# A hybrid decoder layer: the second tiles' turns through three PSUM banks, w_down differences tied to the products, attention's groups of products kept whole

## The chip, the cores and the metric

The kernel runs on one core of one Trainium2 chip. The time is that of one execution on the device, in microseconds, as the median of a few runs. Engines are named as in the profile: PE is TensorE (matrix products), PEld its weight loads, DVE is VectorE, ACT is ScalarE, POOL is GpSimd, SP is SyncE, which issues most DMA transfers.

## The reference, cut to what matters

One layer on 2048 tokens of width 1024, all float32: attention in a window of 128 tokens and a convolution group side by side, one output projection, then a gated feed-forward network of width 2816.

```python
h = x
hn = rms_norm(h, mix_pre_g)
proj = hn @ w_in                       # q (8 heads of 64), k, v (2 heads), u
attn_out = sliding_window_attention(q, k, v, attn_sinks, rel_bias)
conv_out = conformer_conv(u, conv_dw, conv_dw_b, conv_ln_g, conv_ln_b, w_conv_pw)  # width 31
mixed = jnp.concatenate([attn_out, conv_out], axis=-1) @ w_out
h = h + rms_norm(mixed, mix_post_g)
hn = rms_norm(h, ffn_pre_g)
ff = (jax.nn.silu(hn @ w_gate) * (hn @ w_up)) @ w_down
h = h + rms_norm(ff, ffn_post_g)
```

Inside the attention, for each block of 128 queries: scores against 256 keys (the block before and its own), a bias by distance, a mask, a softmax with a sink for each head, and the product with the values.

## The kernel before

The 2048 tokens are four tiles of 512. A float32 operand of a product is split into a rounded part and a rest (ACT writes the first, a subtraction on DVE the second), and a product is three: first by first, first by rest, rest by first. That is why products come in threes and twelves.

The stages, by the letter behind the @ in a tile's name, with the tile's number (A1 is stage A of tile 1): A projects the inputs, tile by tile; B is attention; C is the convolution, whose 31 taps are multiply-adds on DVE; U folds the pointwise weight into the output projection; W is the output projection and the norm behind it. The feed-forward network works on pairs of tiles (0 with 1, 2 with 3) and by Strassen's scheme: seven products of half size for eight. H makes its operands from the normed rows: for the first tile of a pair plain (`stage_h_plain`), for sums and differences of the quarter blocks in `stage_h_sums`, which needs the second tile's rows too. F makes gate and up: first those of the seven products that need no sums (`stage_pre`; some results are stored in `keeps` and loaded again to seed a bank, line 939), then the others (`stage_p1`), which can start when the operand sums and the first weight sums are there. G is the product with w_down (`stage_p2`). Its weights need differences of w_down's blocks. `stage_tsums` makes the first four of them ahead of time: it loads four blocks (line 1106), subtracts on DVE, and stores the results (line 1112), all its transfers on POOL's queue, in eleven sets.

Attention takes one tile in four blocks. `front` makes the scores of a block in two halves: twelve products of half the array's rows (64 x 128, for two heads at a time) into two banks of PSUM, then a masked copy and two reductions for each bank on DVE. `back` of the block before turns the probabilities on PE (line 491), ACT takes them out of PSUM, POOL cuts them to the window (line 494), and four products of half the array's columns (128 x 64) make the output.

PSUM has eight banks: four named mm for the big products, three named tr, and one named ct. Attention's scores, turns and outputs use tr in rotation. The turns of the normed rows (`turn_row`, eight a tile, four transposes each, line 816) use ct; ACT empties the bank behind each.

A scheduler sets each engine's order at build time. It knows the dependencies, follows a timeline of its own with estimated times, and of the instructions that are ready takes the one with the lowest priority number, which is by default the place in the program's text. Lanes (`Lane.pump`) pull a step of a side stage (attention, taps, tail, operand sums, w_down differences) into the text of the main stage whenever it has gained credit. `tc.add_manual_dep` adds a dependency by hand: of the class NoSync it only sets the order, of the class Sync the engine also waits for it on the chip. The taps were already tied to products in that way (`dve`). Each engine runs its list in order.

Of the kernel before, what the change touches and what calls it, by code (L numbers as in the profile page):

```python
# [37 lines left out]
def layer_kernel(ctx, tc, x, xT, cols, rows, sinks, relb, onehot, w_in, w_pw, w_out, w_gate, w_up, w_down, out):  # L38
    nc = tc.nc
# [21 lines left out]
    def f2(tag, shape=(P, T)):  # L61
        return t_(tag, shape)
# [110 lines left out]

    def after_first(first, r):
        tc.add_manual_dep(
            r.ins,
            first.ins.name,
            mybir.DependencyInfo(mybir.DependencyClass.NoSync, mybir.DependencyReason.DATA),
            reason="both halves of the array start together",
        )  # L180
# [62 lines left out]
    hT = [dr.tile([KC, P, T], F32, name=f"hT{i}") for i in range(2)]  # L243
    qs = {}
    started = set()

# [75 lines left out]
    def stage_a(t, hn, before_kv, hooks, post=None):  # L322
# [79 lines left out]
        for i in range(4):  # L402
# [9 lines left out]
            if post:  # L412
                qt = f2("fa")
                stt(qt, oq, 0.125, rb, ALU.mult, ALU.mult)
                act(qi[:, 0], qt, AF.Copy)
                vtt(qi[:, 1], qt, qi[:, 0].bitcast(F32), ALU.subtract)
            else:
                act(qi[:, 0], oq, AF.Copy, scale=0.125)
                stt(qi[:, 1], oq, 0.125, qi[:, 0].bitcast(F32), ALU.mult, ALU.subtract)
            q.append(qi)  # L420
            yield 5.2
            step(10 + i)
        qs[t] = q

    def stage_b(t):
# [3 lines left out]
        def front(b):  # L429
# [6 lines left out]
            for ip in range(2):  # L436
                os = [tr().rearrange("p (j k) -> p j k", j=2) for _ in range(2)]
                lead = []
                for j in range(2):
                    i = 2 * ip + j  # L440
                    for n, (a, k) in enumerate(((0, 0), (0, 1), (1, 0))):
                        for g in (1, 0):
                            sl = slice(64 * g, 64 * g + 64)
                            r = mat(os[g][:, j], q[i][sl, a, tok], kz[sl, k, win], start=n == 0, stop=n == 2)
                            if lead:
                                after_first(lead[-1], r)
                            if len(lead) < 2:
                                lead.append(r)
                for g in range(2):
                    prev = neg.unsqueeze(2).to_broadcast([P, 2, P]) if first else os[g][:, :, 0:P]  # L450
                    nc.vector.copy_predicated(os[g][:, :, P:], upper.unsqueeze(1).to_broadcast([P, 2, P]), prev)
                    for j in range(2):
                        h = 4 * g + 2 * ip + j
                        nc.vector.tensor_tensor_reduce(
                            out=pr[:, h],
# [24 lines left out]
        def back(b):  # L480
# [3 lines left out]
            for g in range(2):  # L484
# [8 lines left out]
                for kb in range(1 if first else 0, 2):  # L493
                    nc.gpsimd.affine_select(  # L494
                        out=pg[:, kb].rearrange("p (i q) -> p i q", q=P),
# [11 lines left out]
            o = tr()  # L507
            lead = None
            for kb in (1,) if first else (1, 0):
                for g in (1, 0):  # L510
                    sl = slice(64 * g, 64 * g + 64)
                    r = mat(o[sl], vtok[:, b + kb, sl], pt[g][:, kb], start=kb == 1, stop=first or kb == 0)
                    if lead is None:
                        lead = r
                    else:
                        after_first(lead, r)
            at = f2("at")
            act(at, o, AF.Copy)
# [5 lines left out]

        live = {}
        for b in range(5):
            if b < 4:
# [284 lines left out]
    def turn_row(w, xs, k, u):  # L812
        lab[0] = f"H{w}"
        b = ct()
        for s in range(4):
# [283 lines left out]
    def stage_tsums(td):  # L1099
        L = "G0"  # L1100
        for pr in range(NF // 2):
# [248 lines left out]
    RP = 0.1  # L1350
    TIE = 5
    AHEAD = 3
    PRES = {0: 20, 2: 16}
# [172 lines left out]
```

## Time and profile before

| what | value |
|---|---|
| median of 3 runs | 1982.09 us (1979.29 to 1984.77) |
| the profiled execution | 1987.9 us, span 1986.2 us |
| PE busy | 1930.4 us, 97% |
| DVE, ACT, POOL busy | 74%, 48%, 15% |
| mean granted clock of PE | 0.987 of full speed |

The profile is of one execution. "Busy" is the time in which an engine carried out instructions; a row of the timeline gives start, duration, engine, line, operation, output <- inputs, shape of the tile in the array, and the number of like instructions in a row, and in brackets the idle time ahead of it and what ended it. A row of the windows gives start:end and length, then busy time and number of instructions of PE, PEld, DVE, ACT and POOL, then the mean granted clock, the busy share of the DMA engines, and GB/s. A row of the waits gives the engine's instruction and what it waited for: us in total, times, longest. Attention runs from about 98 to 590 us, the first half's F stage from about 600 to 1010, its G stage to about 1320, the second half's F and G stages from there to the end.

### The profile page before, as it was taken

Reading aid. Unit: us, or ns where it says so; the run is one execution under the profiler, and the core shown is the slowest. Engines: PE = TensorE matmul, PEld = TensorE weight load, DVE = VectorE, ACT = ScalarE, POOL = GpSimd, SP = SyncE. Lnnn points to the kernel's source line nnn. Section 1 sums busy time; section 2 is a strip of 40 time slices with the busy share of each in tenths; the row PEclk is TensorE's granted clock in tenths of the full one; section 3 lists DMA queues with packets and bytes.
Section 4 is the critical chain, followed back from the end, with each engine's and each line's share of the span. In section 5 each row is a group of like instructions: output and inputs, shape, how many; then the busy total and the mean of one; then the engine's idle time right before and its main releaser. Section 6 shows DMA issues by size and latency. Waiting matters only on the chain.

```text
span 1986.2 us, 26652 instructions
## 1 busy us (share of the span) xinstructions
PE 1930.4 (97%) x8730; PEld 1546.7 (78%) x8730; DVE 1476.3 (74%) x2648; ACT 961.8 (48%) x1886; POOL 304.3 (15%) x427
## 2 busy tenths in 40 slices
PE   8999999999999699999999999999899999999997
PEld 6877777777777588778888878887688888888886
DVE  5999969995874899787759965666866775555557
ACT  5455354447647544334345464656533433345443
POOL 4011011111121101220000110000023332311003
PEclk9999999999999799999999999999899999999999
DMA  8787657566658668775478777759844542375664
GB/s 311 251 303 219 210 187 256 185 212 214 225 195 281 232 218 266 260 266 184 130 253 276 259 255 242 249 202 309 293 140 169 179 140 96 132 244 181 211 195 144
DMA packets 209578, 435.67 MB, mean 219 GB/s; under 512 B 21752, under 2 KB 39328, under 8 KB 209440
## 3 DMA queue, kind: packets, MB, share of 16 engines
q1 hardware_dynamic: 191648, 402.52, 60.7%
q0 software_dynamic: 7040, 23.07, 3.5%
q10 hardware_dynamic: 10752, 8.39, 1.3%
q8 instruction: 68, 1.11, 0.2%
q14 instruction: 70, 0.57, 0.1%
HBM read 323.26 MB, written 110.63 MB: 218 GB/s over the span
## 4 chain that ended last, share of the span: by engine, by line
PE 77%; DVE 8%; DMA 7%; issue 3%; POOL 2%; ACT 2%; SPq 0%; DVEq 0%; POOLq 0%; ACTq 0%
PE mm@F L85 32%; PE mm@G L85 16%; PE mm@A L85 15%; PE mm@W L85 4%; PE tr@B L85 4%; PE tr@W L85 2%; DVE fc@C L94 2%; DMA wx@G<-w_down 1%; DMA gb@F<-keeps 1%; PE mm@U L85 1%; DVE w@F L94 1%; DVE hl@G L94 1%; PE tr@B L491 1%; DMA td<-wx@G 1%; DMA fc@G<-w_down 1%
## 5 line engine op out<-in xcount | busy, mean ns | idle before, releaser
L94 DVE SCALAR_TENSOR_TENSOR fc@C<-glu@C,colt,fc@C 128x512 f32<-128x512 f32 x480 | 357.3, 758 | 2.6
L85 PE MATMUL mm@F<-hl@H,w@F 128*128 128x512 f32 x1056 | 261.3, 397 | 10.2 <-ACT mm@F L939 10.2
L85 PEld LDWEIGHTS mm@F<-hl@H,w@F 128*128 128x128 f32 x1056 | 201.0, 192 | 54.6 <-ACT mm@F L939 12.5
L85 PE MATMUL mm@G<-hl@G,hl@G 128*128 128x512 f32 x924 | 227.7, 393 | 1.1 <-DVE hl@G L94 1.1
L821 ACT ACTIVATE w@F<-chl@F 128x512 fp32r<-128x512 f32 x220 | 135.9, 626 | 187.8 <-PE mm@F L85 149.6
L85 PE MATMUL mm@A<-hl@A,w@A 128*128 128x512 f32 x840 | 209.5, 397 | 4.2 <-ACT w@A L127 1.5
L85 PEld LDWEIGHTS mm@G<-hl@G,hl@G 128*128 128x128 f32 x924 | 171.7, 188 | 37.3 <-DVE hl@G L94 1.9
L85 PE MATMUL mm@G<-w@G,hl@G 128*128 128x512 f32 x876 | 199.4, 389 | 0.0
L85 PEld LDWEIGHTS mm@G<-w@G,hl@G 128*128 128x128 f32 x876 | 164.4, 188 | 34.1
L85 PEld LDWEIGHTS mm@A<-hl@A,w@A 128*128 128x128 f32 x840 | 156.6, 189 | 42.9 <-issue 3.3
L94 DVE TENSOR_TENSOR w@F<-chl@F,w@F 128x512 fp32r<-128x512 f32 x198 | 151.4, 768 | 49.0 <-ACT w@F L821 48.8
L85 PE MATMUL mm@F<-mid@H,w@F 128*128 128x512 f32 x528 | 136.5, 398 | 20.3 <-ACT w@F L821 13.3
L85 PEld LDWEIGHTS mm@F<-mid@H,w@F 128*128 128x128 f32 x528 | 101.0, 192 | 43.7 <-ACT w@F L821 14.1
L85 PE MATMUL mm@F<-ql@H,w@F 128*128 128x512 f32 x528 | 130.0, 392 | 0.0
L85 PE MATMUL mm@F<-p@H,w@F 128*128 128x512 f32 x528 | 129.1, 389 | 0.0
L85 PE MATMUL mm@F<-x@H,w@F 128*128 128x512 f32 x528 | 126.9, 391 | 0.0
L85 PEld LDWEIGHTS mm@F<-ql@H,w@F 128*128 128x128 f32 x528 | 99.1, 189 | 20.8
L85 PEld LDWEIGHTS mm@F<-p@H,w@F 128*128 128x128 f32 x528 | 99.1, 188 | 20.6
L85 PEld LDWEIGHTS mm@F<-x@H,w@F 128*128 128x128 f32 x528 | 98.4, 188 | 21.1 <-issue 0.8
L127 ACT ACTIVATE w@A<-raw@A 128x512 fp32r<-128x512 f32 x110 | 67.5, 626 | 92.1 <-PE mm@A L85 62.1
L94 DVE TENSOR_TENSOR w@G<-raw@G,w@G 128x512 fp32r<-128x512 f32 x73 | 52.1, 713 | 73.0 <-ACT w@G L821 71.8
L494 POOL TENSOR_SCALAR_AFFINE_SELECT p@B<-p@B 128x512 f32<-128x512 f32 x62 | 51.7, 843 | 338.4 <-ACT p@B L492 337.1
(314 smaller groups left out, 3290.1 us busy)
## 6 DMA issues: line engine op xcount, KB each, us to landing
mids<-fa@F SPq DMA_DIRECT2D x154, 256.0 KB, 2.7
raw@A<-w_in SPq DMA_DIRECT2D x55, 512.0 KB, 4.6
w@A<-lo_in SPq DMA_DIRECT2D x84, 256.0 KB, 3.3
fc@G<-mids SPq DMA_DIRECT2D x77, 256.0 KB, 3.4
fa@G<-mids SPq DMA_DIRECT2D x75, 256.0 KB, 4.4
gb@F<-keeps SPq DMA_DIRECT2D x72, 256.0 KB, 3.5
w@W<-fold SPq DMA_DIRECT2D x32, 512.0 KB, 5.9
raw@F<-w_gate SPq DMA_DIRECT2D x22, 512.0 KB, 4.0
```

Source lines behind the costliest of these rows:

```text
L85: r = nc.tensor.matmul(*args, **kw)
L94: r = op(*args, **kw)
L127: act(w[:, 0], raw, AF.Copy)
L491: nc.tensor.transpose(o[:, i * P : (i + 1) * P], pr[:, 4 * g + i], ident)
L494: nc.gpsimd.affine_select(out=pg[:, kb].rearrange("p (i q) -> p i q", q=P), in_=pg[:, 1].rearrange("p (i q) -> p i q", q=P), compare_op=AL ...
L821: act(w[:, 0], x, AF.Copy)
```

## The change

It has three parts. The turns of tiles 1 and 3 (`w % 2`) go through the three tr banks rather than through ct. Each of the w_down subtractions gets an order dependency on the last big product that the text holds at that place. And attention's groups are kept together: each group of score products, and each of output products, gets a higher priority by SOON = 100, its first product comes behind the last product of the group before, and waits (Sync) on what would make it stop midway: for a score group the previous half's last reduction of the first bank and, in a tile's first block, the second query split it reads; for an output group the last affine_select.

```diff
+    def after_first(first, r, how="NoSync"):
...
+            mybir.DependencyInfo(getattr(mybir.DependencyClass, how), mybir.DependencyReason.DATA),
...
             for ip in range(2):
...
+                before = group[0]
+                p0 = tc.cur_priority
+                tc.cur_priority = p0 - SOON
...
                             if lead:
                                 after_first(lead[-1], r)
+                            else:
+                                for e, how in ((before, "NoSync"), (scored[0], "Sync"), (None if b else q_ready[t][2 * ip + 1], "Sync")):
+                                    if e is not None:
+                                        after_first(e, r, how)
                             if len(lead) < 2:
                                 lead.append(r)
+                            group[0] = r
+                tc.cur_priority = p0
...
+                        if g == 0 and j == 1:
+                            scored[0] = e
...
+            tc.cur_priority = p0 - SOON
             for kb in (1,) if first else (1, 0):
...
                     if lead is None:
                         lead = r
+                        after_first(group[0], r)
+                        after_first(cut, r, "Sync")
...
     def turn_row(w, xs, k, u):
         lab[0] = f"H{w}"
-        b = ct()
+        b = tr() if w % 2 else ct()
...
-                vtt(o, p_, q_, ALU.subtract)
+                r = vtt(o, p_, q_, ALU.subtract)
+                tc.add_manual_dep(
+                    r.ins,
+                    made["rows"][-1].name,
+                    mybir.DependencyInfo(mybir.DependencyClass.NoSync, mybir.DependencyReason.DATA),
+                    reason="weight differences keep pace with the products",
+                )
...
+    SOON = 100
```

Attention, PE's order around the output products of a block of tile 2 (`tr@B2_605`) and the first score products of the next block (`tr@B2_609` and `tr@B2_610`, with kz for the keys); before:

```order
L85 MATMUL mm@W0_620_3874<-w@W0_616_3846,hl@W0_593_3706 128x512 x3
L85 MATMUL tr@B2_605_3779<-p@B2_587_3673,vtok_112 64x512
L85 MATMUL tr@B2_610_3790<-kz_109,ql@A2_492_3120 128x256
L85 MATMUL tr@B2_605_3779<-p@B2_585_3663,vtok_112 64x512
L85 MATMUL tr@B2_609_3789<-kz_109,ql@A2_492_3120 128x256
L85 MATMUL tr@B2_605_3779<-p@B2_587_3673,vtok_112 64x512
L85 MATMUL tr@B2_610_3790<-kz_109,ql@A2_492_3120 128x256
L85 MATMUL tr@B2_609_3789<-kz_109,ql@A2_492_3120 128x256
L85 MATMUL tr@B2_605_3779<-p@B2_585_3663,vtok_112 64x512
L85 MATMUL tr@B2_610_3790<-kz_109,ql@A2_492_3120 128x256
L85 MATMUL tr@B2_609_3789<-kz_109,ql@A2_492_3120 128x256
L85 MATMUL tr@B2_610_3790<-kz_109,ql@A2_499_3181 128x256
```

and now, the same two groups:

```order
L85 MATMUL mm@W0_639_3973<-w@W0_637_3961,hl@W0_593_3706 128x512
L85 MATMUL tr@B2_605_3779<-p@B2_587_3673,vtok_112 64x512
L85 MATMUL tr@B2_605_3779<-p@B2_585_3663,vtok_112 64x512
L85 MATMUL tr@B2_605_3779<-p@B2_587_3673,vtok_112 64x512
L85 MATMUL tr@B2_605_3779<-p@B2_585_3663,vtok_112 64x512
L85 MATMUL tr@B2_610_3790<-kz_109,ql@A2_492_3120 128x256
L85 MATMUL tr@B2_609_3789<-kz_109,ql@A2_492_3120 128x256
L85 MATMUL tr@B2_610_3790<-kz_109,ql@A2_492_3120 128x256
L85 MATMUL tr@B2_609_3789<-kz_109,ql@A2_492_3120 128x256
L85 MATMUL tr@B2_610_3790<-kz_109,ql@A2_492_3120 128x256
L85 MATMUL tr@B2_609_3789<-kz_109,ql@A2_492_3120 128x256
L85 MATMUL tr@B2_610_3790<-kz_109,ql@A2_499_3181 128x256
```

Before, the eight records of two groups alternate one by one; now the four output products stand in a row, and the twelve score products behind them.

PE's order around the turns of tile 1's rows (`@H1`, one name for each of eight rows; `mm@F0` are the big products of the F stage, three to a row of the list); before:

```order
L85 MATMUL mm@F0_1022_6159<-hl@H0_810_4970,w@F0_1008_6098 128x512 x3
L85 MATMUL mm@F0_1022_6159<-hl@H0_813_4981,w@F0_1008_6098 128x512 x3
L816 MATMUL ct@H1_974_5934<-ident_69,chl@W1_938_5731 128x128
L816 MATMUL ct@H1_974_5934<-ident_69,chl@W1_939_5733 128x128
L816 MATMUL ct@H1_974_5934<-ident_69,chl@W1_940_5735 128x128
L816 MATMUL ct@H1_974_5934<-ident_69,chl@W1_941_5737 128x128
L85 MATMUL mm@F0_1022_6159<-hl@H0_821_5028,w@F0_1008_6098 128x512 x3
L85 MATMUL mm@F0_1028_6191<-hl@H0_802_4927,w@F0_1013_6125 128x512 x3
L85 MATMUL mm@F0_1028_6191<-hl@H0_810_4970,w@F0_1013_6125 128x512 x3
L85 MATMUL mm@F0_1028_6191<-hl@H0_813_4981,w@F0_1013_6125 128x512 x3
L85 MATMUL mm@F0_1028_6191<-hl@H0_821_5028,w@F0_1013_6125 128x512 x3
L85 MATMUL mm@F0_1034_6218<-hl@H0_802_4927,w@F0_1020_6154 128x512 x3
```

and now, from the fourth of the eight turns on:

```order
L85 MATMUL mm@F0_1016_6133<-hl@H0_810_4970,w@F0_1000_6062 128x512
L836 MATMUL tr@H1_979_5962<-ident_69,chl@W1_938_5731 128x128
L836 MATMUL tr@H1_979_5962<-ident_69,chl@W1_939_5733 128x128
L836 MATMUL tr@H1_979_5962<-ident_69,chl@W1_940_5735 128x128
L836 MATMUL tr@H1_979_5962<-ident_69,chl@W1_941_5737 128x128
L85 MATMUL mm@F0_1016_6133<-hl@H0_810_4970,w@F0_1000_6062 128x512
L836 MATMUL tr@H1_981_5969<-ident_69,chl@W1_938_5731 128x128
L836 MATMUL tr@H1_981_5969<-ident_69,chl@W1_939_5733 128x128
L836 MATMUL tr@H1_981_5969<-ident_69,chl@W1_940_5735 128x128
L836 MATMUL tr@H1_981_5969<-ident_69,chl@W1_941_5737 128x128
L836 MATMUL tr@H1_985_5994<-ident_69,chl@W1_938_5731 128x128
L836 MATMUL tr@H1_985_5994<-ident_69,chl@W1_939_5733 128x128
```

Before, the turns 974 and 979 have eight rows, 23 products, between them, and the last turn (`ct@H1_993`) stands beside the product `mm@F0_1081`; now three turns stand together in the product `mm@F0_1016`, and the last two ahead of `mm@F0_1028`.

DVE's order ahead of the first weight of the middle products (`w@F0_1104`; `fa` are results of F products, `@H0` the operand sums, `fc@C2` and `glu@C2` taps, `wx@G0` and `fc@G0` w_down differences); before:

```order
L94 TENSOR_TENSOR mb@H0_1070_6406<-chl@H0_1066_6379,mb@H0_1070_6406 128x512
L94 TENSOR_TENSOR mid@H0_1055_6327<-chl@H0_1036_6239,mid@H0_1055_6327 128x512
L94 TENSOR_TENSOR chl@F0_1102_6596<-chl@F0_1101_6594 128x512
L94 TENSOR_TENSOR chl@H0_1059_6351<-chl@H0_1059_6351,chl@H0_1066_6379 128x512
L94 TENSOR_TENSOR wx@G0_1119_6658<-fc@G0_1121_6660,wx@G0_1119_6658 128x512
L94 TENSOR_TENSOR ql@H0_1071_6409<-chl@H0_1066_6379,ql@H0_1071_6409 128x512
L94 SCALAR_TENSOR_TENSOR fc@C2_1083_6465<-glu@C2_1082_6463,colt_74,fc@C2_1083_6465 128x512
L94 TENSOR_TENSOR p@H0_1077_6436<-chl@H0_1059_6351,p@H0_1077_6436 128x512
L94 TENSOR_TENSOR chl@F0_1103_6599<-raw@F0_1100_6592,chl@F0_1101_6594 128x512
L94 TENSOR_TENSOR chl@F0_1102_6596<-chl@F0_1102_6596,raw@F0_1100_6592 128x512
L94 TENSOR_TENSOR w@F0_1104_6602<-chl@F0_1102_6596,w@F0_1104_6602 128x512
L94 TENSOR_TENSOR fc@G0_1121_6660<-fc@G0_1121_6660,wx@G0_1119_6658 128x512
```

and now:

```order
L94 TENSOR_TENSOR fa@F0_1076_6434<-fa@F0_1076_6434,mm@F0_1075_6420 128x512
L94 TENSOR_SCALAR fc@C2_1083_6465<-glu@C2_1082_6463,colt_74 128x512
L94 TENSOR_TENSOR chl@H0_1059_6351<-chl@H0_1059_6351,chl@H0_1066_6379 128x512
L94 TENSOR_TENSOR w@F0_1092_6517<-raw@F0_1085_6471,w@F0_1092_6517 128x512
L94 TENSOR_TENSOR ql@H0_1071_6409<-chl@H0_1066_6379,ql@H0_1071_6409 128x512
L94 TENSOR_TENSOR p@H0_1077_6436<-chl@H0_1059_6351,p@H0_1077_6436 128x512
L94 TENSOR_TENSOR chl@F0_1102_6596<-chl@F0_1102_6596,raw@F0_1100_6592 128x512
L94 TENSOR_TENSOR chl@F0_1103_6599<-raw@F0_1100_6592,chl@F0_1101_6594 128x512
L94 SCALAR_TENSOR_TENSOR fc@C2_1083_6465<-glu@C2_1082_6463,colt_74,fc@C2_1083_6465 128x512
L94 TENSOR_TENSOR w@F0_1104_6602<-chl@F0_1102_6596,w@F0_1104_6602 128x512
L94 TENSOR_TENSOR fa@F0_1088_6490<-fa@F0_1088_6490,mm@F0_1087_6476 128x512
L94 TENSOR_TENSOR mid@H0_1078_6439<-chl@H0_1059_6351,mid@H0_1078_6439 128x512
```

Before, that weight stands 54 instructions behind the addition `fa@F0_1076` and behind `fa@F0_1088`, `1095` and `1099`; now it stands nine behind `fa@F0_1076` and ahead of the others, and the first w_down subtraction (`wx@G0_1116`) comes 15 rows behind it.

More of the change, by code (lines that the diff above doesn't have):

```diff
@@ L177, in after_first @@
             first.ins.name,
-            mybir.DependencyInfo(mybir.DependencyClass.NoSync, mybir.DependencyReason.DATA),
-            reason="both halves of the array start together",
+            mybir.DependencyInfo(getattr(mybir.DependencyClass, how), mybir.DependencyReason.DATA),
+            reason="products of half the array stand together",
         )
```

15 lines of the change are left out of this document (10 added, 5 removed).

## The prediction

> **What bounds the kernel now.** I read the page first, then the PE timeline for stalls, then windows and waits around each stall.
>
> ```profile
> span 1986.2 us, 26652 instructions
> ...
> PE 1930.4 (97%) x8730; PEld 1546.7 (78%) x8730; DVE 1476.3 (74%) x2648; ACT 961.8 (48%) x1886; POOL 304.3 (15%) x427
> ...
> PE   8999999999999699999999999999899999999997
> ...
> PE 77%; DVE 8%; DMA 7%; issue 3%; POOL 2%; ACT 2%; SPq 0%; DVEq 0%; POOLq 0%; ACTq 0%
> ```
>
> TensorE sets the time: it is busy for 97% and is 77% of the chain that ended last. So a gain must either shorten TensorE's own work or remove one of its pauses. Only two slices dip inside the span, the 14th (about 645 to 695 us) and the 29th (about 1390 to 1440 us). The profiled execution took 1987.9 us, 5.8 above the median of 1982.1; I sum against the former and carry the difference to the latter.
>
> **Attention (98 to 590 us): groups kept whole.** Windows of this stage, then TensorE's pieces on its timeline (start, duration, count):
>
> ```profile
> 98.00:248.00 150.00, 150.00 (x755) 114.83 (x754) 143.70 (x337) 77.09 (x196) 16.82 (x28) 1.00 0.75 245
> 298.00:448.00 150.00, 150.00 (x705) 111.28 (x704) 142.24 (x304) 69.92 (x183) 18.86 (x23) 1.00 0.67 218
> 98.00:590.00 492.00, 492.00 (x2391) 366.82 (x2390) 421.62 (x952) 260.66 (x642) 73.19 (x137) 1.00 0.67 221
> ```
>
> ```profile
> 104.30 0.50 PE L85 MATMUL mm@A<-mid@A,w@A 128*128 128x512 f32 x1
> 104.73 0.38 PE L85 MATMUL tr@B<-kz,ql@A 64*128 64x256 f32 x1
> 105.04 0.50 PE L85 MATMUL mm@A<-mid@A,w@A 128*128 128x512 f32 x1
> ...
> 225.15 1.29 PE L85 MATMUL mm@A<-hl@A,w@A 128*128 128x512 f32 x5
> 226.38 0.97 PE L85 MATMUL tr@B<-kz,ql@A 64*128 64x256 f32 x12
> 227.28 0.96 PE L85 MATMUL mm@A<-hl@A,w@A 128*128 128x512 f32 x3
> ...
> 259.89 1.07 PE L85 MATMUL tr@B<-p@B,vtok 128*64 128x512 f32 x2
> 260.89 0.38 PE L85 MATMUL tr@B<-kz,ql@A 64*128 64x256 f32 x1
> ```
>
> ```profile
> 201.66 1.94 PE L85 MATMUL tr@B<-p@B,vtok 128*64 128x512 f32 x8
> 203.53 1.67 PE L85 MATMUL mm@A<-hl@A,w@A 128*128 128x512 f32 x6
> ```
>
> TensorE never idles here (492.00 of 492.00), so cost is the distance from start to start. A full product costs 0.227: 67 steps of it and a last product of 0.50 make the 15.69 us of the row of 68 below. Twelve score products together take 227.28-226.38 = 0.90, plus 0.09 on the product ahead (225.15 to 226.38 is 1.23, five products are 1.14): 0.99, or 0.08 each. One alone takes 105.04-104.73 = 0.31 and lengthens the product ahead from 0.227 to 0.43. A whole value group (eight records, four products) takes 203.53-201.66 = 1.87, and I give it the same 0.09; one product alone (two records) takes 260.89-259.89 = 1.00, so four alone would be 4.0. These groups are now in 72 score pieces and 29 value pieces, first to last:
>
> ```profile
> L85 PE MATMUL tr@B<-kz,ql@A x384: 272/277/385, 98.4 to 559.9; 64*128 64x256 f32 x192
> L85 PE MATMUL tr@B<-p@B,vtok x124: 592/592/644, 145.5 to 585.7; 128*64 128x512 f32 x124
> ```
>
> Summed start to start, with what they add to the product ahead, the score pieces cost 45.9 us and the value pieces 40.3. After the change the order has 35 score pieces and 16 whole value groups: 32 x 0.99 plus some 0.7 for three splits is 32.4, and 15 x 1.96 plus 1.1 for the short first group is 30.5. That is 86.2-62.9 = 23.3; walking TensorE's two orders with the same step costs gives 22.7 (3.7 of it at 98 to 248 us, 7.7 at 298 to 448). Nothing hides it, since TensorE is the busy engine. What can eat it is that heads wait (Sync) for the last reduction and the last affine_select, with everything behind them on TensorE held. VectorE is 143.70 of 150 and 142.24 of 150 busy, so those stretches could shrink by 6.3 and 7.8 before it is the bound, against 3.7 and 7.7 asked. Bounds: -24 (all), and -11 (only the 22.7-11.4 outside the two stretches). I take **-20**, near the full end, because TensorE waits nowhere in this stage now.
>
> [...]
>
> **The start of the middle products (656 to 697 us).** The second tiles' turns went through one bank, a turn for about each 24 products; the operand sums on VectorE come behind them.
>
> ```profile
> 645.05 0.60 PE L816 MATMUL ct@H<-ident,chl@W 128*128 128x128 f32 x4
> ...
> 650.74 0.60 PE L816 MATMUL ct@H<-ident,chl@W 128*128 128x128 f32 x4
> ...
> 656.80 15.69 PE L85 MATMUL mm@F<-hl@H,w@F 128*128 128x512 f32 x68
> 685.10 1.22 PE L85 MATMUL mm@F<-mid@H,w@F 128*128 128x512 f32 x2 [12.61 <-ACT w@F L821]
> 689.31 2.08 PE L85 MATMUL mm@F<-mid@H,w@F 128*128 128x512 f32 x4 [3.00 <-DVE w@F L94]
> 691.19 2.76 PE L85 MATMUL mm@F<-mb@H,w@F 128*128 128x512 f32 x6
> 693.75 3.55 PE L85 MATMUL mm@F<-ql@H,w@F 128*128 128x512 f32 x12
> ```
>
> ```profile
> 655.73 0.69 DVE L94 TENSOR_TENSOR fa@F<-fa@F,mm@F 128x512 f32<-128x512 f32 x1 [0.89 <-PE mm@F L85]
> ```
>
> ```profile
> 625.00:672.00 47.00, 47.00 (x220) 38.89 (x219) 29.13 (x46) 31.43 (x55) 1.99 (x4) 1.00 0.75 251
> 655.70:688.60 32.90, 18.00 (x78) 14.05 (x77) 32.87 (x55) 16.67 (x28) 4.84 (x9) 0.79 0.68 230
> 672.24:697.14 24.90, 9.29 (x27) 6.69 (x26) 24.90 (x41) 8.97 (x15) 5.38 (x10) 0.59 0.65 218
> ```
>
> The 68 products end at 656.80 + 68 x 0.227 = 672.24. VectorE then is busy without a gap (32.87 of 32.90): sums, taps and w_down differences stand ahead of the weights' splits. The next 24 products (2, 4, 6 and 12) take from there to 697.14, 24.9 us instead of 5.45, most of them at a lower clock (mean 0.59): 19.4 lost. In the new order all second turns are issued within some 27 products, the sums begin about 25 us earlier, and the first weight for the middle products stands nine VectorE instructions behind the fa addition of 655.73; at 32.90/55 = 0.60 us each it is there near 662, ten before TensorE needs it. The w_down differences stand behind it. I take **-18.5** of 19.4; the other end is 0, if VectorE's work is only shifted. The cover: the sums lie in VectorE's gaps of 625 to 672 us, 29.13 of 47 busy. There 37 instructions now stand between two fa additions four blocks apart, a block being the 5.69 from turn to turn above; 37 x 0.60 = 22.2 against 22.8 us of TensorE's time, so that cover is thin. Splits that come late there, and the normed rows' loads asked for sooner, cost 0 to 9 (half of the loss they remove); I put **+4**. The pause near 613 us stays:
>
> ```profile
> 615.53 6.69 PE L85 MATMUL mm@F<-hl@H,w@F 128*128 128x512 f32 x21 [2.14 <-ACT mm@F L939]
> ```
>
> **The w_down differences (800 to 880 us).** Their set of four subtractions waits on VectorE, which is in order, for its loads:
>
> ```profile
> 811.83:826.03 14.20, 9.73 (x35) 7.47 (x35) 14.16 (x23) 4.42 (x8) 4.10 (x8) 0.88 0.76 263
> 875.45 2.43 PE L85 MATMUL mm@F<-ql@H,w@F 128*128 128x512 f32 x10
> 879.40 1.66 PE L85 MATMUL mm@F<-yt@H,w@F 128*128 128x512 f32 x6 [1.53 <-DVE at@F L94]
> ```
>
> ```profile
> DVE wx@G L94 <- DMA wx@G<-w_down: 9.1, 3, 6.5
> ```
>
> 34 products take 14.2 instead of 7.7 us at 812, ten take 3.95 instead of 2.27 at 875: 6.5+1.7 = 8.2 lost. Tied to the products, the sets stand 14 to 46 VectorE rows apart from the end of one to the start of the next (mean 26; before, 14 to 23, mean 18). Eight rows more are about 5 us, against a longest wait of 6.5. I take **-6.5**; ends -8.2, and 0 if the loads are late by as much. The first set's first subtraction, which stood in attention, moves behind the start of the middle products too, and the last ends some 20 us later, still ahead of the down products. Their DMAs are the same number on POOL's queue.
>
> **The second half's seeds (1372 to 1438 us).** The fourth tile's turns move too, and with them two loads of 512 KB on SP's queue, ahead of seeds.
>
> ```profile
> 1372.59:1437.86 65.27, 53.70 (x211) 41.73 (x209) 50.02 (x87) 35.83 (x65) 4.71 (x1) 0.90 0.88 312
> 1430.06 4.64 PE L85 MATMUL mm@F<-mid@H,w@F 128*128 128x512 f32 x10 [2.81 <-DVE w@F L94]
> chl@H<-hT SPq DMA_DIRECT2D x3, 512.0 KB, 4.4
> ```
>
> On its timeline these are 195 products, 44.3 us of work, and turns for about 1.1; 65.3 passed: 19.9 lost, some 7 of it around the late split of 1430, the rest behind seeds that DMA (0.88 busy) brings late. Earlier sums take the latter; two loads of 4.4 us ahead of seeds may add 8.8. I take **-4** (ends -7 and +9).
>
> Sum: -20-18.5+4-6.5-4 = **-45**: 1942.9 for a profiled execution, 1937 for the median.
>
> **The rivals.** [...] B: the start stays late; the turns come sooner but the sums push splits and seeds back where VectorE's cover is 0.6 us, so that half of 18.5 and the differences' gain go: -45+9+6.5 = -29.5, 1953. For it: the 12.61 pause followed a VectorE without a gap. C: the two loads crowd the seeds at 0.88 DMA: -45+13 = -32, 1950. D, slower: each of 48 group heads stalls TensorE for its bank, reduction or affine_select, because the planner's times differ from the chip's. The price is 48 x the wait; it decides from 45/48 = 0.94 us per head, and 1.2 us each give 1937+58 = 1995. The pause of 2.14 above shows that longer ones cost double: 21 products took 6.5 instead of 4.8. Against D: the heads have 2.7 us or more of VectorE work in hand in the new order, except one with 0.6. [...] E: the groups and ties bring waits as long as what they take: no change.
>
> **How the numbers follow.** Forecast 0.58, A 0.13, B 0.13, C 0.08, D 0.06, E 0.02. About 6 us (0.3%) is what a measurement of this kernel can tell from no change. All but D and E are faster: 0.92; E 0.02; D 0.06. The range goes from all ends together, -24-19.4-8.2-6.8 = -58 (1924), with 2 below for the spread of runs, to B with attention at -11 and the seeds unimproved, about -17 (1965).
>
> **What would show it.** Right: score pieces of 12 and value pieces of 8 on TensorE's timeline and no pause before them; the 14th slice at 9 and clock 9; no wait for w_down above 1 us; the 29th slice as it was or better. Wrong: TensorE waiting for VectorE's reductions or for POOL in 98 to 590 us; a pause at the middle products; seeds waited for longer than 20 us in all around 1350 to 1400.

## The result and the profile after

The changed kernel takes 1955.2 us (median of 4 runs, 1951.4 to 1960.1), the kernel before 1983.4 beside it: a ratio of 0.9856 with a 95% interval of 0.9834 to 0.9878, some 28 us less. The forecast was 45 less, 1937, in a range of 1922 to 1965.

The page of the changed kernel, its head, slices and chain:

```profile
span 1949.7 us, 26646 instructions
...
PE 1902.9 (98%) x8730; PEld 1537.4 (79%) x8730; DVE 1475.9 (76%) x2648; ACT 958.6 (49%) x1886; POOL 299.0 (15%) x427
...
PE   8999999999999999999999999998999999999997
...
PE 67%; DVE 15%; DMA 10%; issue 4%; ACT 2%; POOL 2%; SPq 1%; DVEq 0%; POOLq 0%; ACTq 0%
```

The 14th slice is full now; the other dip (the 28th slice, about 1316 to 1365 us) is as it was. TensorE is busy for 27.5 us less, some 23 of them in attention, and VectorE's share of the chain nearly doubled, from 8 to 15%.

Attention, as windows (the first two as before, the last cut to where VectorE is fullest), then TensorE's waits in it, then pieces of its timeline:

```profile
98.00:248.00 150.00, 148.86 (x769) 116.20 (x768) 144.75 (x337) 77.96 (x198) 18.11 (x29) 1.00 0.74 250
298.00:440.00 142.00, 138.72 (x695) 105.76 (x694) 138.73 (x307) 68.73 (x180) 21.58 (x28) 1.00 0.67 215
```

```profile
PE mm@W L85 <- DVE x@W L94: 2.1, 1, 2.1
PE tr@B L85 <- DVE sm@A L94: 1.1, 1, 1.1
PE mm@A L85 <- DVE x@W L94: 0.7, 1, 0.7
```

```profile
374.48 1.94 PE L85 MATMUL tr@B<-p@B,vtok 128*64 128x512 f32 x8
376.35 0.97 PE L85 MATMUL tr@B<-kz,ql@A 64*128 64x256 f32 x12
377.25 4.62 PE L85 MATMUL mm@W<-w@W,hl@W 128*128 128x512 f32 x19
384.01 1.65 PE L85 MATMUL mm@W<-w@W,hl@W 128*128 128x512 f32 x6 [2.15 <-DVE x@W L94]
```

A value group of eight records and a score group of twelve stand whole, at the 1.87 and 0.90 us read before. TensorE waited for nothing here before. Now one wait (1.1 us) is at the head of a group; the others shown are projections that wait for VectorE's additions.

The start of the first half's middle products, and TensorE's window there:

```profile
627.85 25.11 PE L85 MATMUL mm@F<-hl@H,w@F 128*128 128x512 f32 x108 [0.83 <-ACT mm@F L959]
652.80 1.30 PE L85 MATMUL mm@F<-ql@H,w@F 128*128 128x512 f32 x5
...
672.71 2.36 PE L85 MATMUL mm@F<-yt@H,w@F 128*128 128x512 f32 x6 [2.29 <-DVE at@F L94]
674.86 2.45 PE L85 MATMUL mm@F<-mid@H,w@F 128*128 128x512 f32 x6
```

```profile
640.00:690.00 50.00, 46.92 (x199) 37.92 (x198) 46.37 (x76) 23.18 (x42) 8.60 (x16) 0.97 0.80 264
```

The middle products follow at 652.80 without a pause. A smaller one comes 20 us later, where VectorE, busy for 46.37 of 50, is late with an addition. VectorE's waits from 600 to 900 us:

```profile
DVE fa@F L94 <- DMA mids<-fa@F: 10.3, 6, 3.1
DVE wx@G L94 <- DMA fc@G<-w_down: 6.4, 3, 3.2
...
DVE wx@G L94 <- DMA wx@G<-w_down: 1.7, 1, 1.7
```

The longest wait for w_down fell from 6.5 to 3.2 us, and all of them together from 16.2 to 8.1; the sign that the prediction asked for, none above 1 us, did not come. The waits for stores of fa, 2.8 us in the same window before (2.0 in a second look at that kernel), have grown to 10.3. The second half's seeds:

```profile
1341.07 7.57 PE L85 MATMUL mm@F<-hl@H,w@F 128*128 128x512 f32 x24 [2.65 <-ACT mm@F L959]
1353.74 8.43 PE L85 MATMUL mm@F<-hl@H,w@F 128*128 128x512 f32 x24 [5.10 <-ACT mm@F L959]
...
1372.55 23.66 PE L85 MATMUL mm@F<-hl@H,w@F 128*128 128x512 f32 x96 [1.96 <-ACT mm@F L959]
1396.05 2.88 PE L85 MATMUL mm@F<-mid@H,w@F 128*128 128x512 f32 x12
```

Here the middle products (1396.05) start on time too, and the pauses for seeds are longer instead: 12.1 us in all and up to 5.10, where they were 8.1 and the longest 3.3.

To see where time went, I took the starts of the same few products from each trace and list the distance between them (us). The columns are: start of the 341st product of A (before attention's groups); to the last of W; to the 694th of F (over the start of the middle products); to the 1387th of F (over the w_down differences); to the second half's 1849th; to the 2311th (over the seeds); to the end.

```
                      start  attention  mid start  w_down  ...G...  seeds   rest
before                 96.5      475.5      167.9   165.4    416.5  128.2  536.1
before, second look    97.8      475.5      164.8   163.3    417.4  128.4  536.0
after                  97.4      456.8      152.2   162.0    417.3  128.1  536.0
turns alone            97.1      475.5      153.4   164.6    417.3  124.7  536.3
ties alone             97.5      475.6      161.3   166.9    419.2  126.1  536.2
groups alone           97.2      457.9      167.1   167.6    417.4  124.9  536.4
tile 3's turns in ct   97.0      460.4      149.9   162.1    418.3  127.2  536.4
without ties           96.9      460.4      154.2   167.8    417.9  124.9  536.1
without waits          96.9      468.2      152.4   161.7    419.1  125.9  536.1
differences on POOL    97.9      457.7      159.4   178.9    417.3  123.8  536.2
fewer taps             97.0      456.2      149.6   163.1    417.1  127.5  536.2
taps later, t3 in ct   98.7      459.7      149.2   165.5    423.3  130.6  536.2
seeds sooner, t3 in ct 97.4      457.0      147.4   161.3    420.1  128.4  536.4
seeds sooner, t3 in tr 96.4      458.8      146.4   163.5    417.6  118.1  536.2
```

Where attention's groups are as before, and TensorE waits for nothing there, attention takes the same time in every trace (475.5, 475.5, 475.5, 475.6). With whole groups it doesn't: five kernels with one and the same order of TensorE in this stretch (after, tile 3's turns in ct, differences on POOL and both with seeds sooner) take 456.8 to 460.4. Most of that spread stands behind the two longest pauses, where products run at half speed in some traces and not in others (0.43 us apart instead of 0.227); behind the pause at 119 us they do so in tile 3's turns in ct (1.62 us long) and not in the changed kernel (1.14). So the 456.8 of the changed kernel is the shortest of the five. Behind attention a stretch differs by 3 us and more from execution to execution of the same code (the first and the second look at the kernel before: 167.9 and 164.8).

### The profile page after: what moved, and what is told of

It is laid out like the page before. It is cut to its first block, busy times and chain, and to the rows that moved or that the text cites. A ratio compares the mean times of both kernels' runs of the same rounds, so it can differ in the third digit from the quotient of the medians.

```text
span 1949.7 us, 26646 instructions
## 1 busy us (share of the span) xinstructions
PE 1902.9 (98%) x8730; PEld 1537.4 (79%) x8730; DVE 1475.9 (76%) x2648; ACT 958.6 (49%) x1886; POOL 299.0 (15%) x427
## 4 chain that ended last, share of the span: by engine, by line
PE 67%; DVE 15%; DMA 10%; issue 4%; ACT 2%; POOL 2%; SPq 1%; DVEq 0%; POOLq 0%; ACTq 0%
PE mm@F L85 30%; PE mm@G L85 17%; PE mm@A L85 8%; DVE fc@C L94 5%; PE mm@W L85 4%; PE tr@W L85 3%; PE tr@B L85 2%; DMA mids<-fa@F 2%; DVE w@F L94 1%; DMA keeps<-fa@F 1%; DVE chl@F L94 1%; DVE fa@F L94 1%; DMA w@W<-fold 1%; DMA gb@F<-keeps 1%; PE tr@B L504 1%
## 5 line engine op out<-in xcount | busy, mean ns | idle before, releaser
L85 PE MATMUL mm@F<-hl@H,w@F 128*128 128x512 f32 x1056 | 261.1, 398 | 14.8 <-ACT mm@F L959 13.6
L85 PEld LDWEIGHTS mm@F<-hl@H,w@F 128*128 128x128 f32 x1056 | 201.1, 192 | 61.6 <-ACT mm@F L959 17.7
L841 ACT ACTIVATE w@F<-chl@F 128x512 fp32r<-128x512 f32 x220 | 136.3, 626 | 186.3 <-PE mm@F L85 164.8
L507 POOL TENSOR_SCALAR_AFFINE_SELECT p@B<-p@B 128x512 f32<-128x512 f32 x62 | 56.6, 918 | 338.1 <-ACT p@B L505 336.6
```

Of the source, the lines that this page charges most:

```text
L85: r = nc.tensor.matmul(*args, **kw)
L507: cut = nc.gpsimd.affine_select(out=pg[:, kb].rearrange("p (i q) -> p i q", q=P), in_=pg[:, 1].rearrange("p (i q) -> p i q", q=P), compare ...
L841: act(w[:, 0], x, AF.Copy)
```

## The experiments

**One part at a time.** My theory was that the parts add up, each at its place; the rival, that the w_down differences in VectorE's queue, not the sums, made the long pause.

Turns alone:

```diff
 # the kernel before
-        b = ct()
+        b = tr() if w % 2 else ct()
```

> The kernel before with the turns of tiles 1 and 3 in the three tr banks, and nothing else. Theory (the parts add up, each at its place): the middle products of the first half start without the long pause, -14 at 656 to 697 us; the seeds of the second half lose what the earlier sums gain there, 0; attention as before, 0; the w_down waits stay, 0. Sum -14, about 1969. Rival (the w_down differences ahead of the splits were the cause of the long pause): the pause stays mostly, -3, about 1980.

1970.5 us, ratio 0.9936 (0.9920 to 0.9952). The start of the middle products takes 153.4 instead of 167.9, 14.5 less, as the theory had it. The rival falls: three subtractions of w_down still run in the 40 us ahead of the first of the middle products (five before), and the long pause is gone; TensorE's longest wait in this stretch is 1.7 us. The next run is the counterpart: none runs there, and a long pause stays.

Ties alone:

```diff
 # the kernel before
-                vtt(o, p_, q_, ALU.subtract)
+                r = vtt(o, p_, q_, ALU.subtract)
+                tc.add_manual_dep(r.ins, made["rows"][-1].name, ...)
```

> The kernel before with the w_down differences tied to products, and nothing else. Theory: five instructions of 0.60 us less ahead of the first split, 3 us of the long pause, and 3.5 us of the waits at 800 to 880 us: -6, about 1977. Rival: the pause was due to the differences, -14 to -18, about 1967. Third: the waits for w_down only move, with nothing gained, 0.

1984.9 us, ratio 1.0004 (0.9993 to 1.0016): nothing, the third case. The long pause is shorter, 9.60 instead of 12.61:

```profile
681.17 1.22 PE L85 MATMUL mm@F<-mid@H,w@F 128*128 128x512 f32 x2 [9.60 <-ACT w@F L821]
```

The start gains 3.5 to 6.6 us (161.3 against 164.8 and 167.9), about what the theory had for the five instructions, and the next stretch loses 1.5 to 3.6 of it. TensorE's and VectorE's waits there, from 735 to 800 and 700 to 800 us, of this kernel:

```profile
PE mm@F L85 <- DVE at@F L94: 4.0, 2, 3.1
```

```profile
DVE wx@G L94 <- DMA fc@G<-w_down: 4.1, 2, 2.8
DVE fa@F L94 <- DMA mids<-fa@F: 4.0, 2, 3.4
```

The wait for w_down was not taken away but made shorter and moved, TensorE's longest pause there from 818 to 787 us (3.3 and 3.1 us long), and a wait for the stores of fa joined it. At the end this trace is 3.4 us shorter than the first look at the kernel before and 0.4 shorter than the second; by the medians nothing is gained.

Groups alone:

```diff
 # the changed kernel
-        b = tr() if w % 2 else ct()
+        b = ct()
...
-                r = vtt(o, p_, q_, ALU.subtract)
-                tc.add_manual_dep(r.ins, made["rows"][-1].name, ...)
+                vtt(o, p_, q_, ALU.subtract)
```

> The kernel before with attention's groups kept whole, and nothing else. Theory (TensorE's own work shrinks): the score and value pieces, summed start to start, fall from 86.2 to 64 us, and TensorE waits some 4 us for VectorE in 98 to 590 us: -18, about 1965. Rival (VectorE is the bound at a density of 0.96): -11, about 1972, with VectorE at 0.96 or more of each 150 us and TensorE idle for some 11 us there.

1970.9 us, ratio 0.9941 (0.9920 to 0.9961), as the rival had the time. But its reason is not there: attention is 17.6 us shorter in the trace (457.9 against 475.5), as the theory had it. Against the first look the whole trace is as much shorter as attention, 17.7 us. Against the second look, whose time is nearer to the median, 14.7 are left: the start takes 2.3 and the stretch over the w_down differences 4.3 us more, the seeds 3.5 less. VectorE doesn't wait longer for the loads: its waits for w_down from 600 to 900 us are 13.8 us, against 16.2 and 13.4 in the two looks, those for stores of fa 5.2 against 2.8 and 2.0. What makes the two stretches longer stays open, as does whether it is more than their spread. The product of the three ratios is 0.9881, all parts together give 0.9856: within their intervals the parts add up.

**Tile 3's turns back.** Is the second half's zero a gain and a loss that cancel?

```diff
 # the changed kernel
-        b = tr() if w % 2 else ct()
+        b = tr() if w == 1 else ct()
```

> The changed kernel with tile 3's turns back in the ct bank; tile 1's stay in tr. Theory (tile 3's turns bring the first half's gain again, but the loads they set free crowd the seeds, and the two cancel): the pauses for seeds fall by some 7 us, a late split of the middle products comes back with some 7 us; the time as the changed kernel's, 1955, within 3. Rival (the crowding is the larger): 4 to 7 us faster than the changed kernel, 1950. Third (the earlier sums are the larger): 4 to 7 us slower, 1961.

1953.2 us (1951.4 to 1956.1), as the changed kernel. From the same stretch's waits, in this kernel and in the changed one:

```profile
PE mm@F L85 <- ACT mm@F L959: 7.3, 4, 3.0
PE mm@F L85 <- ACT w@F L841: 2.1, 2, 1.7
```

```profile
PE mm@F L85 <- ACT mm@F L959: 12.1, 5, 5.1
```

The seeds' waits fall by 4.8 us and waits for splits of weights come back, less of them (2.1 and 0.5 us) than the theory's 7; the time is the same. But without sooner seeds and with the taps where they were the stretch varies from 123.8 to 128.4, with either place of tile 3's turns, so this alone would not show that the two cancel; the two runs with sooner seeds, below, do.

**Ties in company.**

```diff
 # the changed kernel
-                r = vtt(o, p_, q_, ALU.subtract)
-                tc.add_manual_dep(r.ins, made["rows"][-1].name, ...)
+                vtt(o, p_, q_, ALU.subtract)
```

> The changed kernel without the ties of the w_down differences; the turns and the groups stay. Theory (the ties take away waits for w_down at 800 to 880 us and give most of it back earlier, at 740 to 790, as VectorE waits there for stores of fa): 1 to 4 us slower than the changed kernel, 1957. Rival (the forecast's term: the whole 6.5 is gained): 1962. Third (nothing is gained at all, as with the ties alone): 1955.

1956.7 us, ratio 0.9865 (0.9841 to 0.9888) against 0.9856 with them. The three cases can't be told apart by time: the two ratios differ by 0.0009, and with both intervals that difference is known to some 0.0032, about 6 us, so neither nothing nor the rival's 6.5 is excluded. In the traces the stretch over w_down takes 167.8 without ties and 162.0 with them, and TensorE's waits for the additions (at@F) from 600 to 900 us are 8.1 and 3.7 us, more than the medians show; but the one trace is of the longest of its runs and the other of the shortest.

**The differences on POOL.** VectorE looked like the bound behind the middle products' start.

```diff
 # the changed kernel
-                r = vtt(o, p_, q_, ALU.subtract)
+                r = ptt(o, p_, q_, ALU.subtract)
```

> The changed kernel with the 44 w_down subtractions on POOL in place of VectorE (at 1.4 to 1.5 us each for the like on POOL). Theory (VectorE, busy 0.84 to 0.96 of each 50 us from 640 to 840, is what TensorE waits for there): the pauses from 650 to 870 us, some 8 us with their slow clock, go for the most part: 1948. Rival (stores and loads are late, not VectorE): no change, 1955. Third (POOL's long instructions hold its queue of loads, and the sets end later than the down products want them): slower, 1958 or more.

1973.0 us, ratio 0.9946 (0.9929 to 0.9964): 18 us slower than the changed kernel. The theory falls. The third case had the direction, but its reason, sets that end too late for the down products, does not show: the G stretch takes 417.3 us as in the changed kernel. VectorE's groups by operation from 640 to 870 us, of the changed kernel and then of this one (count | busy, mean ns), and the window of each:

```profile
L94 DVE TENSOR_TENSOR chl@F<-raw@F,chl@F 128x512 f32<-128x512 f32 x34 | 22.5, 681 | 0.0
L94 DVE TENSOR_TENSOR at@F<-at@F,mm@F 128x512 f32<-128x512 f32 x30 | 20.0, 678 | 3.1 <-PE mm@F L85 2.9
```

```profile
640.00:870.00 230.00, 223.54 (x972) 182.54 (x971) 205.02 (x333) 92.83 (x164) 38.84 (x72) 0.99 0.75 251
```

```profile
L94 DVE TENSOR_TENSOR chl@F<-raw@F,chl@F 128x512 f32<-128x512 f32 x30 | 25.8, 889 | 0.0
L94 DVE TENSOR_TENSOR at@F<-at@F,mm@F 128x512 f32<-128x512 f32 x26 | 17.3, 682 | 5.0 <-PE mm@F L85 5.0
```

```profile
640.00:870.00 230.00, 215.09 (x901) 174.47 (x900) 208.56 (x275) 89.06 (x158) 87.05 (x104) 0.96 0.71 241
```

VectorE is busy for 208.56 us with 275 instructions, where it was for 205.02 with 333. The mean of 889 ns hides two kinds: 7 of the 30 `chl@F<-raw@F,chl@F` overlap a subtraction on POOL and take 1564 ns on average, the other 23 take 684. The five `at@F<-at@F,mm@F` that overlap one, with an input in PSUM, take 683. Besides, without VectorE in the way the sets start sooner, and their transfers meet the seeds: from 600 to 660 us POOL's queue moves 6.02 MB instead of 0.12, a seed's load takes 5.1 us to land instead of 4.6 (medians), and TensorE waits 9.8 us for seeds from 600 to 950, against 1.5. What the move was to bring stays open, since both costs may hide it.

**Fewer taps.** Does VectorE's load eat the rest of attention's gain?

```diff
 # the changed kernel
-                stt(y, g[:, j : j + T], dwh[:, c, j : j + 1], y, ALU.mult, ALU.add)
+                if t != 1 or j % 8 != 7:
+                    stt(y, g[:, j : j + T], dwh[:, c, j : j + 1], y, ALU.mult, ALU.add)
```

> The changed kernel with 12 of the 120 tap multiply-adds of tile 1 left out (three for each block of channels), so its convolution is incomplete. It takes some 8 to 9 us of VectorE's work out of attention, most of it from 298 to 440 us, where VectorE is busy for 138.7 of 142. Theory (VectorE is what eats the rest of the attention gain): the pauses at 362 to 384 us, 4.3 in all, go, and attention ends 4 us sooner: 1951. Rival (the pauses come from the order of the heads, not from VectorE's load): they stay, 1955.

1948.4 us (1945.9 to 1950.9), 7 less than the changed kernel, but not where the theory had it: attention takes 456.2 instead of 456.8, and the pauses have moved rather than gone. TensorE's longest waits there:

```profile
PE mm@A L85 <- DVE x@W L94: 2.3, 1, 2.3
PE tr@B L85 <- DVE sm@A L94: 1.3, 1, 1.3
```

From 298 to 440 us VectorE is busy for 127.25 of 142 us now instead of 138.73, and the longest pause is no shorter (2.3 against 2.1). So in this range it is not VectorE's fullness that sets these waits. That they come from where an instruction stands in VectorE's order is the likely reason; no run moved one instruction alone. The 7 us are not put down to anything.

**The kernel before, again**, with no edit:

> The kernel before, a second look. Theory (its first profile was of a long run, 4.9 us above the median of 17): attention takes the 475.6 us of the first profile within 0.5, and what is shorter lies behind 600 us, in the pauses at 613, 672, 811 and 1375 to 1435. Rival: attention itself varies by several us, so that the gain of 17 us seen there is partly chance.

1985.0 us, a single run. Attention takes 475.5 us in both looks, as the theory had it, so the gain there is no chance. The second look is 3 us shorter: 5.2 less between 572 and 905 us, 2.2 more elsewhere.

**Order without waits.**

```diff
 # the changed kernel
-  ((before, "NoSync"), (scored[0], "Sync"), (None if b else q_ready[t][2 * ip + 1], "Sync"))
+  ((before, "NoSync"), (scored[0], "NoSync"), (None if b else q_ready[t][2 * ip + 1], "NoSync"))
...
-                        after_first(cut, r, "Sync")
+                        after_first(cut, r)
```

> The changed kernel with the three waits at the heads of attention's groups turned into mere order (NoSync); priority and chain stay. The order then has 54 score pieces in place of 35 and 16 value pieces as before. Theory (a piece more costs some 0.36 us of TensorE's time, (45.9-32.4)/37): attention 5 to 7 us longer, 1961. Rival (the heads' waits cost what the whole groups save): attention as long or shorter, 1955 or less, with the pause at 118 us gone.

Attention takes 468.2 us, 11.4 more than in the changed kernel and 8 to 11 more than in the five traces with its order: the waits at the heads hold the score groups together and cost less than they save. The rival falls, though the pause at 118 us is gone as it had it. The 54 score pieces, summed start to start, take some 40 us instead of 33 to 34, within the 5 to 7 of the theory. Of the other 5, some 2 are one more output group (eight records, 1.87 us) that falls into the stretch in this order. They are not new waits: from 95 to 575 us TensorE waits 3.5 us here and 4.5 in the changed kernel. The rest stays open. The time is 1957.5 (1956.8 to 1962.0), only 2.3 above the changed kernel: its profile is of the longest run, and what the other runs make good I can't see.

**Seeds sooner.** From tile 3's turns I went on to what the second half waits for.

```diff
 # the changed kernel, with tile 3's turns in ct
-                kept[q] = f2("gb")
+                kept[q] = f2("at" if q % 2 else "gb")
...
-            fetch(q + 2)
+            if q + 3 == PRE:
+                fetch(q + 2)
+            fetch(q + 3)
```

> The changed kernel with tile 3's turns in ct, and the seeds' loads asked for one product sooner, in turn into the buffers gb and at (four in place of two). Theory (the loads wait because DMA is full, 0.9 and more busy at 330 to 350 GB/s from 1336 to 1376 us, so asking sooner moves the waits and takes away a little): the seeds' waits fall from 11 to about 8 us, 2 to 3 us gained, 1951. Rival (they wait for their buffers): the pauses around 1340 to 1375 go for the most part, 12 to 15 us gained with their slow clock, 1940. Third: loads pushed ahead of others delay the weights' loads, slower, 1957.

1947.9 us, ratio 0.9816 (0.9792 to 0.9839). TensorE waits for no seed any more in the second half, as the rival had it, but the time is not the rival's. DMA's part, as windows of the changed kernel and then of this one:

```profile
1286.00:1336.00 50.00, 50.00 (x239) 41.55 (x238) 39.09 (x99) 41.13 (x87) 0.00 (x0) 1.00 0.88 304
1336.00:1376.00 40.00, 27.94 (x92) 20.50 (x91) 37.04 (x71) 22.83 (x41) 0.00 (x0) 0.84 0.91 330
```

```profile
1286.00:1336.00 50.00, 50.00 (x231) 41.16 (x230) 41.97 (x113) 43.60 (x91) 0.00 (x0) 1.00 0.96 335
1336.00:1374.00 38.00, 38.00 (x175) 31.39 (x173) 20.69 (x34) 21.30 (x36) 0.00 (x0) 1.00 1.01 382
```

The 330 GB/s are a mean over full and empty parts: from 1336 to 1366 us, where the longest pauses for seeds are, the changed kernel's DMA is full too (share 1.00, 366 GB/s), as the theory read it. It has room in the 50 us before (0.88), and there the kernel with sooner loads moves more (0.96). The likeliest reading is that both hold in part: DMA is full when the seeds are due, and two buffers keep them from being asked for earlier. The edit changes the buffers and the asking together, so it does not tell these apart. But the sums are late now (TensorE's timeline):

```profile
1364.68 9.68 PE L85 MATMUL mm@F<-hl@H,w@F 128*128 128x512 f32 x42
1389.77 1.22 PE L85 MATMUL mm@F<-mid@H,w@F 128*128 128x512 f32 x2 [15.41 <-ACT w@F L841]
```

It is the pause that the first half had, behind the turns in one bank, and it takes back what the seeds gave: the stretch is no shorter (128.4 against 127.2). What this kernel gains over its base lies in part in the first half, where the edit holds too (the start takes 147.4 instead of 149.9).

**Taps later.**

```diff
 # the changed kernel, with tile 3's turns in ct
-    RC0, RC1, RC2, RC3, RW0, RW, RB, LC = 0.7, 1.1, 0.4, 0.9, 1.7, 1.25, 0.8, 100
+    RC0, RC1, RC2, RC3, RW0, RW, RB, LC = 0.7, 0.8, 0.4, 0.9, 1.7, 1.25, 0.8, 100
```

> The changed kernel with tile 3's turns in ct, and tile 1's taps asked for at a rate of 0.8 in place of 1.1, which moves some of them out of 298 to 440 us, where VectorE is full, into 440 to 500, where it is not. Theory (the pauses at 362 to 384 us are those of a full VectorE): they go, 3 us gained, 1950. Rival (as leaving taps out showed, they move to other places with the order): within 2 us of 1953. The order has 33 score pieces and 16 value pieces, as the base within two.

1965.8 us, 12.6 above its base, and both expectations fall. Attention is no shorter (459.7 against 460.4), now with a wait of 3.0 us for POOL at a value group; the three stretches over w_down, G and the seeds are longer by 3.4 to 5 us, perhaps because the taps stand there now. The planner's order answers to such a number as a whole, so this run does not test the one cause it was made for.

**Both.**

```diff
 # the changed kernel (tile 3's turns in tr), and the seeds' loads as two runs above
+            fetch(q + 3)
```

> The changed kernel, tile 3's turns in tr as it has them, with the seeds' loads asked for one product sooner into gb and at in turn. Seen in the run before: with tile 3's turns in ct the sooner seeds take away the seeds' pauses, but the middle products of the second half then start 15.8 us late behind the operand sums. Theory (the two pauses share one stretch of full DMA, and turning tile 3 early is worth something once the seeds no longer wait): the pause at about 1374 us shrinks to 3 to 8 us, 1938 to 1943. Rival (DMA is simply full there, so what one load gains another loses): the pause returns at the seeds or the weights, 1948. Third (the two loads of the sums crowd seeds and weights as before): 1952 or more.

1939.6 us (1937.1 to 1943.8), ratio 0.9779 (0.9760 to 0.9797): faster than the kernel before and the changed one, as the theory had it. Its timeline at the same place:

```profile
1330.08 27.32 PE L85 MATMUL mm@F<-hl@H,w@F 128*128 128x512 f32 x119
...
1380.88 0.73 PE L85 MATMUL mm@F<-mid@H,w@F 128*128 128x512 f32 x2 [4.51 <-ACT w@F L841]
```

The pause at the middle products is 4.5 us instead of 15.4, and the stretch takes 118.1 instead of 128. Turning tile 3 early is worth 8 (by the medians) to 10 us (by the traces), once the seeds no longer wait.

## Why the prediction was right, and where it was not

Direction and range held; the size was 28 for a forecast of 45, so the time lies nearer to rival B's 1953 and C's 1950 than to the forecast. The stretches tell what the time does not. By the forecast's steps:

- **Attention, -20: right in mechanism and nearly in size.** The trace gives -18.7 (475.5 to 456.8), of the 22.7 in the orders; over all nine kernels with whole groups and waits at the heads it was between 15 and 19, so that -18.7 is at the good end. The pieces shrank as worked out, and some 4 us of new waits, nearly all for VectorE, took the rest. VectorE as the bound of attention at the density it had before, 0.96 (A among the chances, -11, 1946), did not come: it was busy for 138.73 of 142 us, denser than that, and with taps left out (127.25 of 142) the waits stayed. Of the waits, those of 2.1 and 0.7 us are for additions x@W, which empty banks of full products and not of those of half the array.
- **The start of the middle products, -18.5 and +4: right.** -15.7 against the first look and -12.6 against the second, for a net -14.5; turns alone bring it (153.4). The thin cover held with two pauses of about 0.8 and one of 2.3 us.
- **The w_down differences, -6.5: the step that missed most.** The stretch is 1.3 to 3.4 us shorter than in the two looks. Alone the ties are worth nothing (1.0004); in company they are worth between nothing and the whole term, which the runs can't narrow (0.9856 and 0.9865). The step took eight VectorE rows more between sets as 5 us off each wait and looked for no other wait. The waits for w_down did halve, but VectorE then waited 10.3 us for the stores of fa. These two waits trade places: in the two kernels with sooner seeds, with the same ties, they are 12.4 and 14.8 us for w_down and 5.0 and 4.6 for the stores (600 to 900 us), and TensorE waits there no longer than in the changed kernel. What decides between them stays open.
- **The seeds, -4: 0.** The late split went as forecast (-7), and longer waits for seeds took it back: rival C's mechanism, though it cost the gain and no more. Full DMA was read as the cause of these waits. It was full at the longest of them (share 1.00 from 1336 to 1366 us) but had room in the 50 us before (0.88), and asking sooner, with four buffers for two, took the waits away.
- **The base.** The sum was made against one execution of 1987.9, 4.5 above the median of 1983.4, and the changed kernel's profile is 3.8 below its own. Trace against trace the change is 36.5 us, with the medians 28. The forecast carried the first offset over unchanged; but what made that execution long lay at least partly behind attention, in stretches with pauses that the change removes or shortens (the second look is 5.2 us shorter over the start and w_down), and the median run can't gain it. Against the second look the trace is 33.5 us shorter, and what the forecast lacks there is 5.2 us at w_down, 3.7 at the seeds, 1.9 at the start and 1.3 in attention; the last 5 us are that the second look was 1.5 above its median and the changed kernel's trace 3.8 below.
- **D**, stalls at the heads, did not come: one head of 48 waits 1.1 us, and without the waits attention is longer. **B**: pauses behind the start are there (2.29 us at 672), but the start took 12.6 to 15.7 us less, so its nearness in time is chance.

## What to carry to other kernels

Changes between products of the whole array and of half of it were a cost of the order here, not of the work (8730 TensorE instructions in both kernels, and attention took 456.8 us instead of 475.5): count the pieces, price one alone and in a group (a score product took 0.08 us in a group of twelve; alone 0.31, and the product ahead 0.20 more), and let the first of a group wait for everything the group needs. A stage that started late because its inputs came through a ring of one buffer was repaired by a ring of three, and showed its gain in one half only when the next wait in the same stretch was repaired too: the same edit was worth 14 us in one half and nothing in the other, until the seeds were asked for sooner. Sum a change against medians of several profiles where pauses are part of it: in two executions of the kernel before, attention, without pauses, took 475.5 us both times, and the start, with them, 167.9 and 164.8.

## What the runs showed of the hardware that was not expected

- A subtraction on POOL slowed VectorE's work beside it: a group with both inputs in SBUF rose from 681 to 889 ns on average, because the few instructions that overlap one took 1564 and the others 684; with one input in PSUM it stayed at 678 to 682. The one group with both inputs in SBUF that did not rise (chl@F<-chl@F,raw@F, 15 instructions, 686 ns) overlaps no subtraction at all.
- After most pauses of 2 us and more TensorE's full products stood 0.43 us apart instead of 0.227, at a granted clock of 0.50 (before from 617.0 to 619.4 us, behind the pause of 2.14; after from 1355 to 1358, behind that of 5.10). By the idle times of all 14 traces from 95 to 1900 us, 31 of 32 pauses of 2.4 to 3.4 us that full products follow have 7 to 14 products at 0.43 us close behind (the exception is 2.50 us at 1415 in groups alone). Of 18 pauses of 1.9 to 2.4 us 11 have them (2.14 at 615 before) and 7 don't (2.15 at 743 in fewer taps), and of 57 pauses of 1.0 to 1.9 us four. By these counts a pause of 2.5 us costs about 4, as an estimate: seven products at 0.20 us more add 1.4.
